# Choosing which partitions stay empty in a row gather with duplicates removed

## The chip, the cores and the metric

The kernel runs on one core of a Trainium2 chip. The metric is the device time of one execution in microseconds. The core has five compute or control engines, PE (TensorE), DVE (VectorE), ACT (ScalarE), POOL (GpSimd) and SP (SyncE), and 16 DMA engines that move data between HBM and the on-chip memory of 128 partitions.

## The reference

```python
def setup_inputs():
    batch, seq, dim = 32, 512, 1024
    return {
        "x": np.random.randn(batch, seq, dim).astype(np.float32),
        "indices": np.random.randint(0, seq, (batch, 128)).astype(np.int32),
    }

def reference(x, indices):
    result = np.zeros((batch, indices.shape[1], x.shape[2]), dtype=np.float32)
    for b in range(batch):
        result[b] = x[b, indices[b]]
    return result
```

For each of 32 batches, 128 rows of 1024 float32 (4 KB each) are copied from 512 rows, chosen by an index that may name a row more than once. The draw is fixed: batches have between 109 and 120 different rows among their 128, the last one (batch 31) 113.

## The kernel before, in words

The output is 32 blocks of 128 rows, one per batch, each written by a store of 512 KB that SP issues (`store`, L137 to L142; batches 12 to 19 are stored in pairs, 1 MB each). Input rows come by indirect DMAs that POOL issues (`gather`, L121, one per batch, 128 slots, one slot per partition).

Batches 0 to 4 (`HEAD`) are gathered directly, duplicates included, into `block` tiles and stored. Batch 0 takes its indices from `first`, a small transfer of one column; batches 1 to 4 take them from `idxT`, the transposed indices, which PE and DVE make out of `vals` by way of `vf` (L94 to L113).

Batches 5 to 31 are handled in nine groups of three. For these, each different row is fetched once. DVE and PE work out, in three steps per group (`step0`, `step1`, `step2`):

- `cnt`: how many earlier places in the batch name the same row. `lead` marks the places with none, that is the first mention of each row.
- `past` and `nth`: the running number of a leading place. It counts on through the batches, modulo 128, so that the run of numbers that a batch does not use moves on from batch to batch.
- `pack`: which partition (slot) takes which leading place. A slot p takes the place whose number equals `turn[p]`, a fixed permutation of 0 to 127 that is the same in all partitions and comes from the iotas of `rank` (L73 to L79, turned to float16 at L93).
- `at`: the row index that each slot fetches. A slot that no place claims gets 1024, beyond the limit of the gather's bounds check, and fetches nothing.
- `s`: a 0/1 matrix with which PE later spreads the fetched rows to all places that name them.

The gather for such a batch goes into one of eight ring tiles `u` (`RING`, L207 to L215; ACT clears them once at the start, since empty slots keep what is there). PE multiplies `s` with the tile in two halves of 512 columns, ACT copies each half from PSUM to the batch's block, and SP stores the block (`spread_rows`, L238 to L247). The gather eight batches later is then issued. Batch 5 also uses 256 rows that two plain loads (`early`) bring ahead; its gather fetches only rows from 256 on.

Each engine's instructions keep the order in which the code emits them: a helper (`InOrder`, L13 to L25) chains the operations of PE, DVE and ACT, which is why most rows of the profile carry L21 or L24. POOL and SP work through their DMA issues in order. Waits between engines are semaphores that the framework sets. The DMA engines serve the queues of stores (q1, issued by SP), gathers (q0, issued by POOL), the loads by ACT (q10) and two queues marked "instruction" (q8, q14).

Of the kernel before, what the change touches and what calls it, by code (L numbers as in the profile page):

```python
# [7 lines left out]
F16 = mybir.dt.float16  # L8
I32 = mybir.dt.int32
ALU = mybir.AluOpType  # L10
# [18 lines left out]
def kernel(ctx, tc, x, indices, out):  # L29
# [11 lines left out]

    nc = tc.nc
    B, S, D = x.shape
    N = indices.shape[1]
    HEAD, RING, GROUP, AHEAD, FAR = 5, 8, 3, 4, 1024
    HALF = HEAD
    PAIRED = range(12, 20)
    GROUPS = (B - HEAD) // GROUP  # L50
    assert 2 * N <= S <= FAR and (B - HEAD) % GROUP == 0
    const = ctx.enter_context(tc.tile_pool(name="const", bufs=1))
# [8 lines left out]
    pe, dve, act = InOrder(tc), InOrder(tc), InOrder(tc)  # L61
    mm, v = nc.tensor.matmul, nc.vector
# [7 lines left out]

    diff = const.tile([N, N], I32, name="diff")
    nc.gpsimd.iota(diff[:], pattern=[[1, N]], base=0, channel_multiplier=-1)
    rank = const.tile([N, 8, 16], I32, name="rank")  # L73
    for e in range(8):
        fold = 0
        for bit, col in enumerate((6, 5, 3)):
            fold ^= col * (e >> bit & 1)
        steps = [[(-16 if fold >> bit & 1 else 16) << bit, 2] for bit in (2, 1, 0)]
        nc.gpsimd.iota(rank[:, e], pattern=[[1, 2]] + steps, base=2 * e + 16 * fold, channel_multiplier=0)  # L79
    less = const.tile([N, 1], F32, name="less")  # L80
    zero = const.tile([N, 1], F32, name="zero")
    dve(v.memset, zero[:], 0.0)
# [6 lines left out]
    dve(v.tensor_copy, out=less[:], in_=diff[:, 0:1])  # L89
    every = const.tile([N, N], F16, name="every")  # L90
    dve(v.memset, every[:], 1.0)
    turn = const.tile([N, N], F16, name="turn")
    dve(v.tensor_copy, out=turn[:], in_=rank[:].rearrange("p e q -> p (e q)"))  # L93
    vf = const.tile([N, N], F16, name="vf")  # L94
    dve(v.memset, vf[:], 0.0)
    dve(v.tensor_copy, out=vf[:B],
        in_=vals[:].bitcast(I32).rearrange("p (n two) -> p n two", two=2)[:, :, 0])


    xf = x.flatten_outer_dims()  # L100
# [47 lines left out]
    def table(name, dtype):  # L148
        return const.tile([N, B], dtype, name=name)

    cnt, lead, slot = table("cnt", F32), table("lead", F16), table("slot", F16)
    nth, at = table("nth", I32), table("at", I32)
    past = const.tile([N, B + 1], F16, name="past")
    dve(v.memset, past[:, HEAD:HEAD + 1], 0.0)
    bcs, packs, spread = {}, {}, {}

    def of_group(g):
        return range(HEAD + g * GROUP, HEAD + (g + 1) * GROUP)

    def cols(t, g):  # L160
        return t[:, HEAD + g * GROUP:HEAD + (g + 1) * GROUP]

    def wide(t):
        return t.rearrange("p (g o) -> p g o", o=1).to_broadcast([N, GROUP, N])

    def step0(g):

        bcs[g] = bc = pbc.tile([N, 4, N], F32, name="bc")
        for k, b in enumerate(of_group(g)):
            pe(mm, bc[:, k], lhsT=ident[:, b:b + 1].to_broadcast([N, N]), rhs=vf[:], start=True, stop=True)  # L170
        for k, b in enumerate(of_group(g)):
            junk = junkp.tile([N, N], F16, name="junk")
            dve(v.scalar_tensor_tensor, out=junk[:], in0=bc[:, k], scalar=idxF[:, b:b + 1], in1=below[:],
                op0=ALU.is_equal, op1=ALU.mult, accum_out=cnt[:, b:b + 1])
        if HALF in of_group(g):
            c = slice(HALF, HALF + 1)
            dve(v.scalar_tensor_tensor, out=cnt[:, c], in0=idxF[:, c], scalar=2.0 * N, in1=cnt[:, c],
                op0=ALU.is_lt, op1=ALU.add)
        dve(v.tensor_scalar, out=cols(lead, g), in0=cols(cnt, g), scalar1=0.0, scalar2=None, op0=ALU.is_equal)
        for b in of_group(g):  # L180
            dve(v.tensor_tensor, out=past[:, b + 1:b + 2], in0=past[:, b:b + 1], in1=lead[:, b:b + 1], op=ALU.add)

    def step1(g):

        rk = psm.tile([N, GROUP], F32, name="rk")
        pe(mm, rk[:], lhsT=above[:], rhs=cols(lead, g), start=True, stop=False)
        pe(mm, rk[:], lhsT=every[:], rhs=cols(past, g), start=False, stop=True)
        dve(v.tensor_copy, out=cols(nth, g), in_=rk[:])
        dve(v.tensor_scalar, out=cols(nth, g), in0=cols(nth, g), scalar1=N - 1, scalar2=None, op0=ALU.bitwise_and)
        dve(v.scalar_tensor_tensor, out=cols(slot, g), in0=cols(cnt, g), scalar=256.0, in1=cols(nth, g),  # L190
            op0=ALU.mult, op1=ALU.add)
        packs[g] = pack = junkp.tile([N, GROUP, N], F16, name="pack")
        dve(v.tensor_tensor, out=pack[:], in0=turn[:].rearrange("p (o n) -> p o n", o=1).to_broadcast([N, GROUP, N]),
            in1=wide(cols(slot, g)), op=ALU.is_equal)

    def step2(g):

# [40 lines left out]
    def spread_rows(b):  # L238
# [8 lines left out]
        store(b)  # L247

    step0(0)
    step0(1)  # L250
    for g in range(AHEAD):
        step1(g)
        if 0 < g < AHEAD - 1:
            step0(g + 1)
        step2(g)
        for b in of_group(g):
            if b < HEAD + RING:
                fetch(b)
        if g == 0:
            half_spread()  # L260
        elif g < 3:
            half_rows(g - 1, False)
    for b in range(HEAD, B):
        spread_rows(b)
        fetch(b + RING)
        g, step = divmod(b - HEAD, GROUP)
        if g + AHEAD < GROUPS:
            (step0, step1, step2)[step](g + AHEAD)
# [30 lines left out]
```

## Time and profile before

| what | value |
|---|---|
| median of 9 runs | 88.55 us (87.98 to 89.06) |
| the profiled execution | 88.22 us |
| its span | 86.4 us |
| PE / DVE / ACT / POOL busy | 72% / 37% / 47% / 39% of the span |
| bytes moved by DMA | 32.91 MB, mean 381 GB/s |
| gathers of batches 5 to 31 | 27 issues, 11.7 us from issue to landing (median) |
| stores | 24 of 512 KB (9.2 us to landing), 4 of 1 MB (12.8 us) |

The span is the time from the first instruction to the end of the last one in the profiled execution; its own time also counts what lies around it. A busy share is an average over the whole span. The DMA row of the profile gives, for 40 equal slices, how much of the 16 DMA engines' time was taken, in tenths, and the GB/s row what they moved. The DMA queue rows give packets, megabytes and the time that the packets took as a share of 16 engines' span. In the tables by stretches, the columns are the stretch, its length, the busy time of PE, weight loads, DVE, ACT and POOL with the number of instructions, then PE's granted clock, the DMA share and GB/s. A timeline row has start, duration, engine, line, operation, what it writes and reads, and in brackets how long the engine had been idle before it and what ended that.

### The profile page before, as it was taken

The page shows a single profiled execution, that of the slowest core. Times are in us where ns is not written, and L with a number is a line of the kernel's source. Part 1 is how long each engine was busy: PE and PEld are TensorE (multiplying, and loading weights), DVE is VectorE, ACT ScalarE, POOL GpSimd, SP SyncE. Part 2 cuts the span into 40 slices and gives each one's busy share as a digit, 9 for nine tenths or more (in the row PEclk, how much of TensorE's full clock was granted, in tenths as well). Part 3 has the DMA queues.
Part 4 walks back from the last instruction along what each step waited for, and adds up shares of the span by engine and source line. Part 5 has one row for each costly group of instructions (what it writes and reads, how often), then busy time and mean ns, then how long its engine had stood idle before and what let it go on. Part 6 is the DMA issues. An engine that isn't in the chain of part 4 may idle for free.

```text
span 86.4 us, 829 instructions
## 1 busy us (share of the span) xinstructions
PE 61.9 (72%) x189; PEld 25.4 (29%) x189; DVE 31.6 (37%) x160; ACT 40.5 (47%) x63; POOL 33.5 (39%) x45
## 2 busy tenths in 40 slices
PE   0040169596799999999999999777798888785000
PEld 0030133151345444443444443222133333220000
DVE  3289895592565486473754850000000000000000
ACT  0999910000165665566566555555434454455000
POOL 7557587737144555554445555433200000000000
PEclk9999999999999999999999999999999999999955
DMA  0998999999999999999999999999999999999970
GB/s 1 256 408 271 328 334 336 415 421 419 415 415 421 421 419 419 415 421 417 419 417 410 415 423 421 421 419 413 417 423 421 413 419 419 421 419 421 417 324 9
DMA packets 9636, 32.91 MB, mean 381 GB/s; under 512 B 1584, under 2 KB 1616, under 8 KB 9632
## 3 DMA queue, kind: packets, MB, share of 16 engines
q1 hardware_dynamic: 4736, 16.81, 47.9%
q0 software_dynamic: 4608, 15.01, 44.6%
q10 hardware_dynamic: 288, 1.05, 3.4%
q8 instruction: 1, 0.02, 0.1%
q14 instruction: 3, 0.02, 0.1%
HBM read 17.86 MB, written 16.78 MB: 401 GB/s over the span
## 4 chain that ended last, share of the span: by engine, by line
PE 40%; DMA 23%; issue 13%; DVE 9%; POOL 5%; ACT 1%; POOLq 1%; SPq 0%; DVEq 0%
PE ps L24 38%; DMA u<-in_x_dram,at 19%; POOL u L122 5%; DMA vals<-in_indices_dram 3%; DVE junk L24 2%; DVE nth L24 1%; DVE pack L24 1%; DVE past L24 1%; PE pos L24 1%; PE bc L24 1%; DVE slot L24 1%; ACT block L246 1%; DVE s L24 1%; DVE same L24 1%; SPq L66 0%
## 5 line engine op out<-in xcount | busy, mean ns | idle before, releaser
L24 PE MATMUL ps<-u,s 128*128 128x512 f32 x108 | 51.9, 610 | 4.7 <-DMA u<-in_x_dram,at 4.6
L122 POOL DMA_INDIRECT u<-in_x_dram,at x27 | 26.9, 997 | 24.5 <-PE bc L24 6.1
L246 ACT COPY block<-ps 128x512 f32<-128x512 f32 x36 | 21.1, 585 | 18.4 <-PE ps L24 16.8
L24 PEld LDWEIGHTS ps<-u,s 128*128 128x128 f32 x108 | 18.3, 189 | 26.4 <-ACT block L246 14.7
L246 ACT COPY pair<-ps 128x512 f32<-128x512 f32 x16 | 9.4, 585 | 5.9 <-PE ps L24 4.2
L24 DVE SCALAR_TENSOR_TENSOR junk<-bc,idxF,below 128x128 f16<-128x128 f32 x27 | 8.0, 347 | 6.2 <-PE bc L24 6.2
L24 ACT COPY u<-zero 128x1024 f32<-128x1024 f32 x8 | 7.7, 1038 | 0.0
L24 PE MATMUL ps<-early,same 128*128 128x512 f32 x8 | 7.3, 1064 | 0.0
L236 ACT COPY block<-ps 128x512 f32<-128x512 f32 x2 | 1.2, 585 | 12.5 <-PE ps L24 12.5
L24 PE MATMUL pos<-near,pack 128*128 128x1 f16 x27 | 2.0, 167 | 5.5 <-DVE pack L24 3.3
L24 DVE TENSOR_TENSOR pack<-turn,slot 128x384 f16<-128x384 f16 x9 | 5.0, 558 | 0.3
L24 DVE TENSOR_TENSOR s<-bc,at 128x384 f32<-128x384 f32 x9 | 5.0, 558 | 0.3
L24 DVE TENSOR_TENSOR past<-past,lead 128x1 f16<-128x1 f16 x27 | 4.4, 164 | 0.9
L122 POOL DMA_INDIRECT block<-in_x_dram,idxT x4 | 3.8, 946 | 1.9 <-DVE past L24 1.0
L24 PEld LDWEIGHTS <-pack 128*128 128x128 f16 x27 | 1.7, 100 | 9.5 <-DVE pack L24 4.8
L24 PE MATMUL bc<-vf,ident 128*128 128x128 f16 x27 | 3.4, 256 | 1.3 <-issue 1.3
L24 PEld LDWEIGHTS <-ident 128*128 128x128 f16 x27 | 2.4, 111 | 4.2 <-issue 4.2
L21 PE MATMUL pos<-ident,vf 128*128 128x32 f16 x1 | 0.2, 207 | 4.2 <-DVE vf L24 4.2
L24 DVE TENSOR_SCALAR at<-pos 128x3 int32<-128x3 f32 x9 | 1.4, 160 | 4.2 <-PE pos L24 3.8
L24 PEld LDWEIGHTS ps<-early,same 128*128 128x128 f32 x8 | 2.4, 324 | 2.1 <-issue 2.1
L24 DVE CAST nth<-rk 128x3 int32<-128x3 f32 x9 | 1.4, 159 | 3.9 <-PE rk L24 3.2
L24 ACT ACT_TABLE_LOAD x1 | 1.3, 1283 | 2.2 <-DVE ident L24 2.2
(31 smaller groups left out, 18.0 us busy)
## 6 DMA issues: line engine op xcount, KB each, us to landing
out_dram<-block SPq DMA_DIRECT2D x24, 512.0 KB, 9.2
out_dram<-pair SPq DMA_DIRECT2D x4, 1024.0 KB, 12.8
early<-in_x_dram ACTq DMA_DIRECT2D x2, 512.0 KB, 3.8
u<-in_x_dram,at POOLq DMA_INDIRECT x27, 11.7
block<-in_x_dram,idxT POOLq DMA_INDIRECT x4
vals<-in_indices_dram SPq DMA_DIRECT2D x1, 32.0 KB
first<-in_indices_dram SPq DMA_DIRECT2D x1, 1.0 KB
block<-in_x_dram,first POOLq DMA_INDIRECT x1
```

The costliest lines, as they stand in the source:

```text
L21: self.last = do(*args, **kw)
L24: self.last = do(*args, **kw)
L122: nc.gpsimd.indirect_dma_start(out=dst, out_offset=None, in_=xf[:], in_offset=bass.IndirectOffsetOnAxis(ap=at, axis=0), element_offset=b * ...
L236: nc.scalar.copy(out=blocks[HALF][:, w], in_=ps[:])
L246: nc.scalar.copy(out=blocks[b][:, w], in_=ps[:])
```

## The change

Two things are done to the permutation, and a few small ones follow.

First, `turn` is made from another formula. The new `rank[:, 0]` gives partition p the number 64 * ((p >> 5) & 1) + 16 * (p & 3) + 8 * (p >> 6) + ((p >> 2) & 7): numbers that follow one another belong to different values of 8 * (p >> 6) + ((p >> 2) & 7). In the old one they belong to different values of p >> 3.

Second, the last batch has a permutation of its own, `rank[:, 1]`, and its counting restarts at 0 (`past` of batch 31 is cleared). Numbers 112 to 123 lie at partitions 36 to 47, numbers 124 to 127 at partitions 104 to 107. The batch uses numbers 0 to 112, so its 15 empty slots are partitions 37 to 47 and 104 to 107.

The eight iotas of 16 elements for `rank` become one of 128 and five of 36, 12, 56, 4 and 20. The conversion to `turn` is 256 wide instead of 128 and comes after `vf` instead of before it. A second column of `past` is cleared at the start, and two additions to `past` in the last group are left out. The last group's `pack` is made by two instructions, one for two batches and one for the last.

```diff
-    rank = const.tile([N, 8, 16], I32, name="rank")
-    for e in range(8):
-        fold = 0
-        for bit, col in enumerate((6, 5, 3)):
-            fold ^= col * (e >> bit & 1)
-        steps = [[(-16 if fold >> bit & 1 else 16) << bit, 2] for bit in (2, 1, 0)]
-        nc.gpsimd.iota(rank[:, e], pattern=[[1, 2]] + steps, base=2 * e + 16 * fold, channel_multiplier=0)
+    rank = const.tile([N, 2, N], I32, name="rank")
+    nc.gpsimd.iota(rank[:, 0], pattern=[[8, 2], [64, 2], [1, 8], [16, 4]], base=0, channel_multiplier=0)
+    for p0, p1, at0 in ((0, 36, 0), (36, 48, 112), (48, 104, 36), (104, 108, 124), (108, N, 92)):
+        nc.gpsimd.iota(rank[:, 1, p0:p1], pattern=[[1, p1 - p0]], base=at0, channel_multiplier=0)
...
-    turn = const.tile([N, N], F16, name="turn")
-    dve(v.tensor_copy, out=turn[:], in_=rank[:].rearrange("p e q -> p (e q)"))
     vf = const.tile([N, N], F16, name="vf")
...
+    turn = const.tile([N, 2, N], F16, name="turn")
+    dve(v.tensor_copy, out=turn[:], in_=rank[:])
...
-    dve(v.memset, past[:, HEAD:HEAD + 1], 0.0)
+    for b in (HEAD, B - 1):
+        dve(v.memset, past[:, b:b + 1], 0.0)
...
         for b in of_group(g):
-            dve(v.tensor_tensor, out=past[:, b + 1:b + 2], in0=past[:, b:b + 1], in1=lead[:, b:b + 1], op=ALU.add)
+            if b < B - 2:
+                dve(v.tensor_tensor, out=past[:, b + 1:b + 2], in0=past[:, b:b + 1], in1=lead[:, b:b + 1], op=ALU.add)
...
-        dve(v.tensor_tensor, out=pack[:], in0=turn[:].rearrange("p (o n) -> p o n", o=1).to_broadcast([N, GROUP, N]),
-            in1=wide(cols(slot, g)), op=ALU.is_equal)
+        like = GROUP - (g == GROUPS - 1)
+        dve(v.tensor_tensor, out=pack[:, :like], in0=turn[:, 0:1].to_broadcast([N, like, N]),
+            in1=wide(cols(slot, g))[:, :like], op=ALU.is_equal)
+        if like < GROUP:
+            dve(v.tensor_tensor, out=pack[:, like:], in0=turn[:, 1:2], in1=wide(cols(slot, g))[:, like:], op=ALU.is_equal)
```

## The prediction

> **What bounds the kernel now.** I read the slices and the DMA queues of the page first, then the busy time by stretches, then the stretches at the end, because a change of 15 transfer slots can only show where one DMA engine ends last.
>
> ```profile
> span 86.4 us, 829 instructions
> DMA  0998999999999999999999999999999999999970
> GB/s 1 256 408 271 328 334 336 415 421 419 415 415 421 421 419 419 415 421 417 419 417 410 415 423 421 421 419 413 417 423 421 413 419 419 421 419 421 417 324 9
> q1 hardware_dynamic: 4736, 16.81, 47.9%
> q0 software_dynamic: 4608, 15.01, 44.6%
> q8 instruction: 1, 0.02, 0.1%
> q14 instruction: 3, 0.02, 0.1%
> ```
>
> The DMA row is at 9 from the third slice to the last but one: the 16 engines together are the bound, and the 72% of PE is cover. q1 carries the stores, q0 the gathers. Two small queues carry instructions. The stretches say it in shares:
>
> ```profile
> 6.00:8.00 2.00, 0.33 (x2) 0.10 (x1) 1.79 (x13) 2.00 (x3) 1.53 (x2) 1.00 0.81 252
> 10.00:12.00 2.00, 0.48 (x3) 0.21 (x2) 1.90 (x8) 1.16 (x2) 1.12 (x2) 1.00 0.94 287
> 20.00:76.00 56.00, 50.38 (x151) 20.52 (x149) 18.48 (x86) 29.54 (x51) 20.51 (x21) 1.00 1.03 418
> ...
> 82.00:83.00 1.00, 0.00 (x0) 0.00 (x0) 0.00 (x0) 0.00 (x0) 0.00 (x0) 0.50 1.00 410
> 83.50:84.00 0.50, 0.00 (x0) 0.00 (x0) 0.00 (x0) 0.00 (x0) 0.00 (x0) 0.50 0.55 221
> 84.20:84.40 0.20, 0.00 (x0) 0.00 (x0) 0.00 (x0) 0.00 (x0) 0.00 (x0) 0.50 0.06 21
> 84.60:84.80 0.20, 0.00 (x0) 0.00 (x0) 0.00 (x0) 0.00 (x0) 0.00 (x0) 0.50 0.05 20
> 84.80:85.00 0.20, 0.00 (x0) 0.00 (x0) 0.00 (x0) 0.00 (x0) 0.00 (x0) 0.50 0.05 20
> ```
>
> The last two columns are DMA share and GB/s. From 20 to 76 us the share is 1.03 (records of one engine overlap a little), so no engine waits. At the end it falls to 0.05 to 0.06, which is 1/16: for most of a microsecond **one engine works alone**. The packet records behind these rows give the sixteen completion marks of the last store: fifteen between 83.30 and 84.31 us, the sixteenth at 85.19. The span ends 1.24 us after it.
>
> Why is one engine late? The DMA queues in 46 to 48 us, and in 38 to 40 us:
>
> ```profile
> q8 instruction: 1, 0.02, 2.9%
> q14 instruction: 1, 0.01, 1.0%
> ```
>
> 2.9% of 16 engines times 2 us is 0.93 us for one packet (16,384 bytes, 942 ns in the records); 1.0% is 0.32 us (8,192 bytes, 309 ns). Three of the latter lie in the span, at 14.2, 39.4 and 58.5 us. A 4 KB row costs 4096 bytes / (420 GB/s / 16) = 0.156 us, so the large fetch costs its engine six rows, a small one two. I followed each engine's packets by their end-to-start times (a packet starts 3 or 4 ns before the one ahead of it ends): the last engine's chain to the end begins where the 942 ns packet ends. A skipped slot shows there as a 4-byte packet of 9 ns instead of a 159 ns row.
>
> [...]of the final stretches that I could follow without a break, five match one engine (or a pair that it can't tell apart) exactly; dealing eight neighbouring partitions to each engine misses each by one to three. The 30 gather packets ahead of the 942 ns fetch fit engine 10 alone; those ahead of the fetch at 39.4 us fit engine 2 or 0. [...]
>
> **The change part by part.**
>
> *Ordinary batches.* Old and new `turn` both spread a run of up to 16 consecutive empty ranks over the engines. I counted, from the draw, the empty slots by engine: 432 in batches 5 to 31. The old table gives every engine 27. Before the last batch the new one gives 26 or 27. Nothing to gain here: 0.00 us; its cover is a ring of eight gathers, with the DMA share at 1.03.
>
> *The last batch.* It has 113 different rows of 128, so 15 empty slots. Old: one on each engine but 15. New: rank restarts at 0, ranks 113 to 127 lie at partitions 37 to 47 and 104 to 107, that is three on engine 1 and four each on 2, 3 and 10. Totals become 29 on engine 1, 30 on 2, 3 and 10, 27 on 15, 26 on the others. So engine 10 moves 30 - 27 = 3 rows less: 3 x 0.156 = **-0.47 us**. An engine with 26 moves one row more: +0.16. Is that the new end? The best of the rest ended at 84.31; plus 0.16 is 84.47, and engine 10 comes to 85.19 - 0.47 = 84.72. It stays last, so the whole 0.47 counts. The ceiling is 85.19 - 84.47 = 0.72.
>
> *The start.* The iotas of `rank` took 1.26 us for eight; now one of 128 elements (the `diff` iota let the next start after 0.20) and five at about 0.157: 0.99. POOL would be free at 2.03, not 2.30, but the first gather waits for the `first` transfer until 2.76: nothing. `turn` becomes 256 wide and moves behind `vf`, ahead of `idxT`:
>
> ```profile
> 2.33 0.23 DVE L24 CAST turn<-rank 128x128 f16<-128x128 int32 x1 [0.58 <-POOL rank L79]
> 3.94 0.21 DVE L24 CAST vf<-vals 32x128 f16<-32x128 int32 x1 [1.30 <-DMA vals<-in_indices_dram]
> 4.45 0.19 DVE L24 CAST idxT<-pos 128x32 int32<-128x32 f32 x1 [0.30 <-PE pos L21]
> 4.79 0.06 DVE L24 MEMSET past<- 128x1 f16 x1
> 4.91 0.95 POOL L122 DMA_INDIRECT block<-in_x_dram,idxT  x1 [1.03 <-DVE past L24]
> ```
>
> DVE idles 0.30 us ahead of `idxT`, waiting for PE. `below`, also 128 wide, let its successor start 0.14 after it, so 256 wide is about 0.28 of DVE; it begins between 4.08 and 4.15 and ends its claim at 4.36 to 4.43, just inside 4.45. Bounds: no delay, or 0.06 if only the record's end at 4.15 frees DVE and the full 0.36 counts. The second `past` memset costs 0.05 ahead of the first `junk`, so it delays `at`, the POOL gather queue behind it (first at 10.57) and the DMA engines. At 10 to 12 us these are at 0.94, not full, so a delay there can reach the end. Bounds 0.00 to 0.11; I take +0.03, as part of the engines still have work there.
>
> *The last group.* Its `pack` becomes two instructions (about +0.2 by the short DVE rows at 0.16 to 0.18), two `past` additions go (0.164 each). Its `at` is ready at 51.1 us and its gathers are issued from 55.0 on, when ring tiles and earlier gathers allow: nearly 4 us of cover, 0.00 us. Without it, at most 0.2.
>
> Sum: -0.47 + 0.03 = **-0.44 us**. The profiled execution, 88.22 us with a span of 86.4, would become 87.8; the median of the nine runs is 88.55, 0.33 above it, and would become **88.1**, 0.50% less. About 0.5%, or 0.44 us, is also what a measurement of this kernel can tell from no change.
>
> **The rivals.**
>
> *The late engine is not helped.* If the 16 KB fetch is on an engine outside the four, [...]that engine has 26 empties: +0.16 + 0.03, so 88.7. Against it: the fit to engine 10 and the nearly equal program length.
>
> *The start eats the gain.* If `turn` is dearer than its hole and delays all of the first gathers by 0.2 to 0.3, the result is 88.4. For it: the share of 0.81 at 6 to 8 us shows engines already starved by late gathers. Against it: the hole of 0.30.
>
> *Slower: gathers are dealt by eights.* If the software queue gives engine e the partitions 8e to 8e+7, the new `turn` gathers the empties of a batch on few engines, and totals run from 24 to 36. The last engine, if among the eight with 24, moves three rows more: 88.55 + 0.47 + 0.03 = 89.05. It decides from three rows on; with fewer it stays within 0.5%. [...]
>
> **How the numbers follow.** Relief of engine 10 has 0.66; its centre is on the bound of 0.5%, but a lag that is longer in other executions keeps the gain and a shorter start cost raises it, so 0.49 faster and 0.17 same; its own range is 87.8 to 88.4. Late engine not helped: 0.16 (0.14 same, 0.02 slower). Start eats: 0.10 (0.01 faster, 0.09 same). By eights: 0.08, slower. Sums: 0.50, 0.40, 0.10. The range reaches from the ceiling, 88.55 - 0.72 = 87.8, less 0.2 for the scatter of a median whose runs lie between 87.98 and 89.06, to 88.7 plus the same: 87.6 to 88.9.
>
> **What would show it.** Right: the last completion mark near 84.7, with the stretch at a share of 1/16 shortened from about 0.9 to about 0.25 us; `idxT` still at about 4.45 and the first gather of `u` within 0.1 of 10.57; the small queues still with one packet of 16 KB. Wrong: a lone engine as late as before, two or more engines beyond 84.5 with no large fetch, a steady share under 1.03, or gathers of batches 1 to 4 that begin 0.2 late.

## The result, and the profile after

The changed kernel takes 87.57 us (median of 10 runs, 87.18 to 87.95) beside 88.35 us for the kernel before (31 runs): ratio **0.992**, 95% interval 0.989 to 0.995, that is 0.7 us less (0.5 to 1.0). The forecast was 0.44 us less, 88.1 from 88.55. Ratios and intervals here leave out the executions that took over 1.5% longer than the fastest of the same kernel, so the tables also give the medians of all runs.

The forecast range, 87.6 to 88.9, was set from 88.55; the measured ratio puts 87.8 there, inside it (the median itself, 87.57, stands beside a kernel before at 88.35). Most of the reasoning behind the number did not hold, so that it came out is luck. The first sign is the profiled execution of the changed kernel, which took 88.28 us, no less than the 88.22 of before. Its page answers to the lines shown of before:

```profile
span 86.5 us, 827 instructions
DMA  0797899999999999999999999999999999999980
q8 instruction: 1, 0.02, 0.1%
q14 instruction: 3, 0.02, 0.1%
```

The same one large and three small instruction fetches, and a DMA row that is a little emptier at the start (7, 7 and 8 in the second, fourth and fifth slice, where it was 9, 8 and 9). Then the same stretches (columns as before: the last two are DMA share and GB/s):

```profile
6.00:8.00 2.00, 0.33 (x2) 0.10 (x1) 1.85 (x15) 2.00 (x3) 1.39 (x2) 1.00 0.81 236
20.00:76.00 56.00, 48.30 (x142) 19.94 (x143) 18.20 (x85) 28.13 (x48) 20.98 (x21) 1.00 1.03 418
...
84.20:84.40 0.20, 0.00 (x0) 0.00 (x0) 0.00 (x0) 0.00 (x0) 0.00 (x0) 1.00 0.55 225
84.80:85.00 0.20, 0.00 (x0) 0.00 (x0) 0.00 (x0) 0.00 (x0) 0.00 (x0) 0.50 0.05 20
```

The lone engine at the end (a share of 0.05) now lasts some 0.3 us instead of 0.9: the completion marks of the last store run from 83.93 to 84.80 us, and the sixteenth is at 85.11. So the end is more even, as forecast, though engine 10 is no longer the lone one: by its packets it ends at about 84.5. And the marks' mean is 84.38, against 83.95 before: this execution was already late when it got there. The timeline of its start shows why, and shows a row that the prediction had not asked about:

```profile
1.04 0.50 POOL L76 IOTA rank<- 128x128 int32 x1
1.10 0.48 DVE L24 TENSOR_SCALAR ident<-diff 128x32 f16<-128x32 int32 x1 [0.23 <-POOL diff L74]
1.61 0.38 ACTq L21 DMA_DIRECT2D early<-in_x_dram  x1
4.51 0.22 DVE L24 CAST vf<-vals 32x128 f16<-32x128 int32 x1 [2.46 <-DMA vals<-in_indices_dram]
5.03 0.19 DVE L24 CAST idxT<-pos 128x32 int32<-128x32 f32 x1
5.49 0.95 POOL L121 DMA_INDIRECT block<-in_x_dram,idxT  x1 [1.61 <-DVE past L24]
```

And the rows of the kernel before that answer to it and were not shown:

```profile
1.10 0.18 DVE L24 TENSOR_SCALAR ident<-diff 128x32 f16<-128x32 int32 x1 [0.23 <-POOL diff L72]
1.31 0.38 ACTq L21 DMA_DIRECT2D early<-in_x_dram  x1
```

`ident` takes 0.48 us instead of 0.18, since it runs beside the wide iota of 0.50 us; it ends at 1.58, just after the iota. ACT's `early` loads wait for `ident` (`mark`), so they are issued at 1.61 instead of 1.31. Two streams that meet there are the index block `vals` (32 rows of 1 KB, issued at 1.19) and these loads (4 KB rows). In this execution the block was used at 4.51 us, 0.6 later than in the profile of before: all its rows but one had landed by 2.6 us, and that one, which starts at 4.02 as a 4 KB row of the early loads ends, landed at 4.06. Below, a row like this is called caught. In another execution of the same kernel (the run that stands last below) it looks like this:

```profile
1.61 0.38 ACTq L21 DMA_DIRECT2D early<-in_x_dram  x1
2.97 0.21 DVE L24 CAST vf<-vals 32x128 f16<-32x128 int32 x1 [0.92 <-DMA vals<-in_indices_dram]
4.17 0.95 POOL L121 DMA_INDIRECT block<-in_x_dram,idxT  x1 [0.30 <-DVE past L24]
```

There `vf` starts at 2.97 instead of 3.94 and the gather of batch 1 at 4.17 instead of 4.91, when POOL is through with batch 0. That execution took 87.30 us. So there were two theories to tell apart. **L**: the gain is the relief of engine 10, as forecast. **S**: the gain is made at the start, by an iota that slows a DVE instruction that holds back a load.

### The profile page after: what moved, and what is told of

Read it like the earlier page. It is cut to its first block, busy times and chain, and to the rows that moved or that the text cites. A ratio compares the mean times of both kernels' runs of the same rounds, so it can differ in the third digit from the quotient of the medians.

```text
span 86.5 us, 827 instructions
## 1 busy us (share of the span) xinstructions
PE 61.2 (71%) x189; PEld 25.2 (29%) x189; DVE 31.6 (36%) x160; ACT 40.6 (47%) x63; POOL 33.4 (39%) x43
## 4 chain that ended last, share of the span: by engine, by line
DMA 41%; PE 17%; issue 16%; DVE 16%; POOL 3%; ACT 1%; SPq 0%; POOLq 0%; DVEq 0%
DMA u<-in_x_dram,at 37%; PE ps L24 15%; DVE junk L24 4%; DMA vals<-in_indices_dram 4%; POOL u L121 3%; DVE pack L24 3%; DVE past L24 2%; DVE s L24 2%; DVE nth L24 2%; DVE lead L24 1%; DVE slot L24 1%; ACT block L250 1%; PE pos L24 1%; DVE same L24 1%; SPq L68 0%
## 5 line engine op out<-in xcount | busy, mean ns | idle before, releaser
L24 PE MATMUL ps<-early,same 128*128 128x512 f32 x8 | 5.7, 854 | 0.0
L24 DVE TENSOR_TENSOR pack<-turn,slot 128x384 f16<-128x384 f16 (+2 forms) x10 | 5.1, 518 | 0.3
L24 PEld LDWEIGHTS ps<-early,same 128*128 128x128 f32 x8 | 1.9, 257 | 1.5 <-issue 1.5
```

Source lines behind the costliest of these rows:

```text
L24: self.last = do(*args, **kw)
```

## The experiments

**First four: move the empty slots of the last batch, leave the start as changed.** Each edit is to the second table of the changed kernel (the first shows both lines that go, the other two only what is new); the last run is the changed kernel itself.

```diff
# even: one empty slot on each engine but 0
-    for p0, p1, at0 in (...):
-        nc.gpsimd.iota(rank[:, 1, p0:p1], pattern=[[1, p1 - p0]], base=at0, channel_multiplier=0)
+    nc.gpsimd.iota(rank[:, 1], pattern=[[8, 2], [64, 2], [1, 8], [16, 4]], base=0, channel_multiplier=0)
# on engines 12 to 15 (in place of the same two lines)
+    nc.gpsimd.iota(rank[:, 1], pattern=[[1, N]], base=0, channel_multiplier=0)
# eight on engine 10
-    for p0, p1, at0 in ((0, 36, 0), (36, 48, 112), (48, 104, 36), (104, 108, 124), (108, N, 92)):
+    for p0, p1, at0 in ((0, 38, 0), (38, 45, 113), (45, 72, 38), (72, 76, 120), (76, 104, 65), (104, 108, 124), (108, N, 93)):
```

> The changed kernel with one thing undone: the last batch's 15 empty slots lie one on each DMA engine but engine 0 (the second table repeats the first). The new table of the ordinary batches, the wide conversion and its new place stay. Theory L (the gain is the relief of engine 10, which fetches 16 KB of instructions): no gain is left, ratio to the kernel before 1.000 within 0.003. Rival S (the gain comes from the start or from the new table of the ordinary batches): still about 0.992, as the changed kernel.

> The changed kernel, but the last batch's empty slots lie on engines 12 to 15 (3, 4, 4, 4), none on 1, 2, 3 and 10. Theory L: engine 10 moves one row more than before, +0.16 us, ratio about 1.002 and slower than the kernel with even slots. Rival C (bunching of empty slots helps wherever it is, for example by a shorter landing of the last gather): about 0.992, as the changed kernel.

> The changed kernel, but all eight slots of engine 10 are empty in the last batch, the other seven on engines 1 (2), 2 (4) and 3 (1). Theory L with a fixed order of the other engines: engine 10 ends 8 rows less 1, that is 1.09 us, earlier than with even slots and is no longer last; the end is that of the next engine, so a gain of at most about 0.7 us and ratio 0.990 to 0.992, at best 0.2 us better than the changed kernel. Rival (a straight dose): ratio 0.988.

> The changed kernel once more, on the same chip and with the same runs of before as the three others, for the comparison: 0.992, interval about 0.003 each way. Its trace tells how much of the late start of the profiled execution (index block there at 4.4 instead of 3.8 us) belongs to the change: theory J (scatter of the transfer) expects it near 3.8 us in at least some of the four traces, the rival (the wide iota delays it) at 4.4 in all four.

Measured against the kernel before:

| empty slots of the last batch | ratio | 95% interval | all runs: median us, its ratio to 88.43 |
|---|---|---|---|
| even | 0.9957 | 0.9931 to 0.9983 | 88.13, 0.997 (22 runs) |
| on 12 to 15 | 0.9915 | 0.9883 to 0.9946 | 87.65, 0.991 (8) |
| eight on 10 | 0.9905 | 0.9877 to 0.9934 | 87.99, 0.995 (22) |
| as changed, four on 10 | 0.9907 | 0.9870 to 0.9944 | 87.41, 0.988 (9) |

Theory L fails clearly on the second row: with no empty slot at all on engine 10 the kernel is as fast as with four, where L said slower than before. Eight are no better than four, so no dose of engine 10 is to be seen between none, four and eight. With even slots a gain of 0.4 us stays; L said none and S the whole gain, so this row fits neither. What all four share is the start. Their index blocks were in use at 3.17, 3.28, 4.33 and 3.23 us, so the 4.51 of the first profile was one of the two cases that occur, and the rival "4.4 in all four" fails too.

**Four more: both halves apart, on the kernel before.**

```diff
# last batch alone: a second table, made on POOL in the steady part; start and ordinary batches as before
+            for p0, p1, at0 in ((0, 36, 0), (36, 48, 112), (48, 104, 36), (104, 108, 124), (108, N, 92)):
+                with tc.issue_after(gathers[HEAD + RING].ins):
+                    nc.gpsimd.iota(rank2[:, 0, p0:p1], pattern=[[1, p1 - p0]], base=at0, channel_multiplier=0)
+            dve(v.tensor_copy, out=turn2[:], in_=rank2[:])
+            dve(v.memset, past[:, B - 1:B], 0.0)
... (declarations; and past as in the changed kernel)
+            dve(v.tensor_tensor, out=pack[:, like:], in0=turn2[:], in1=wide(cols(slot, g))[:, like:], op=ALU.is_equal)
# early loads later: wait for the fifth DVE operation instead of the second
-    mark = dve(v.tensor_scalar, out=ident[:], in0=diff[:, :B], scalar1=0, scalar2=None, op0=ALU.is_equal)
+    dve(v.tensor_scalar, out=ident[:], in0=diff[:, :B], scalar1=0, scalar2=None, op0=ALU.is_equal)
...
-    dve(v.tensor_copy, out=less[:], in_=diff[:, 0:1])
+    mark = dve(v.tensor_copy, out=less[:], in_=diff[:, 0:1])
# latest: mark is the copy to turn
```

> The kernel before with the last batch's own table alone (empty slots on engines 1, 2, 3 and 10 as in the changed kernel); the table is made late, in the steady part, so that the start, the narrow iotas and the ordinary batches are those of before. Theory L (the gain is the relief of engine 10): -0.47 us, ratio 0.995. Theory S (the gain is made at the start: the wide iota on POOL slows DVE's ident, the early loads are issued 0.3 us later, at 1.6 instead of 1.3, and the index block lands earlier): 1.000, as the start is that of before. Both together, each with half: 0.995 to 0.997.

> The kernel before with one edit: the early loads wait for the fifth DVE operation (the copy to less, done at about 1.6 us) instead of the second (ident, 1.28), so that they are issued about 0.3 us later, as in the changed kernel. Nothing of the dealing is changed. Theory S: the index block lands near 2.8 us in most executions, the gathers of batches 1 to 4 start up to 0.7 us earlier, ratio 0.994 to 0.996, like the kernel with even slots in the last batch. Theory L: 1.000.

> Both edits on the kernel before: the last batch's own table, made late, and the early loads 0.3 us later. If the gain of the changed kernel is the sum of these two, 0.991 to 0.993, as the changed kernel, with nothing left for the new table of the ordinary batches, the wide conversion or its place. If one of the two does all, as that one alone.

> A larger dose of the second edit: on the kernel before, the early loads wait for the copy to turn (done at about 2.56 us), so they are issued about 1.3 us later than before and mostly after the index block has landed. Theory S: the index block is at 2.8 us in every execution and the scatter of the times falls; the early loads themselves come 1.3 us later, which costs only if batch 5 is waiting for them. Ratio 0.992 to 0.996; 1.000 or more if the idle DMA time ahead of them, 1.0 us, is lost.

| edit on the kernel before | ratio | 95% interval | all runs: median us, its ratio to 88.34 |
|---|---|---|---|
| last batch alone | 0.9986 | 0.9953 to 1.0020 | 88.32, 1.000 (14 runs) |
| early loads 0.3 us later | 0.9878 | 0.9823 to 0.9933 | 87.80, 0.994 (6) |
| both | 0.9921 | 0.9894 to 0.9947 | 87.85, 0.994 (22) |
| early loads 1.3 us later | 1.0020 | 0.9998 to 1.0042 | 88.49, 1.002 (22) |

The dealing of the last batch, which was the whole forecast, is worth 0.1 us or nothing. One changed wait, in a kernel whose dealing is untouched, gives a gain (0.994 to 0.996 was expected of it). By the ratios it is the gain of the changed kernel; by the medians of all runs it is 0.5 us, where the changed kernel has 0.8 to 1.0 in its three measurements (0.991, 0.988, 0.989). Whether something else adds to it there, or rows are caught less often there, the runs do not show. The timelines of the second and the fourth show the mechanism and its other side:

```profile
1.64 0.38 ACTq L21 DMA_DIRECT2D early<-in_x_dram  x1
3.27 0.21 DVE L24 CAST vf<-vals 32x128 f16<-32x128 int32 x1 [0.64 <-DMA vals<-in_indices_dram]
4.25 0.95 POOL L122 DMA_INDIRECT block<-in_x_dram,idxT  x1 [0.37 <-DVE past L24]
```

```profile
2.60 0.38 ACTq L21 DMA_DIRECT2D early<-in_x_dram  x1
3.21 0.21 DVE L24 CAST vf<-vals 32x128 f16<-32x128 int32 x1 [0.58 <-DMA vals<-in_indices_dram]
4.19 0.95 POOL L122 DMA_INDIRECT block<-in_x_dram,idxT  x1 [0.31 <-DVE past L24]
```

In both the index block is in use by 3.3 us and the gathers of batch 1 start at 4.2. But with the loads at 2.60 the DMA engines have too little to do from 2 to 4 us. The stretches of the second kernel, then of the fourth:

```profile
2.00:4.00 2.00, 0.46 (x6) 0.46 (x7) 0.73 (x6) 1.45 (x2) 1.43 (x3) 1.00 0.69 238
6.00:8.00 2.00, 0.00 (x0) 0.00 (x0) 1.79 (x13) 2.00 (x3) 1.40 (x2) 1.00 0.91 299
```

```profile
2.00:4.00 2.00, 0.52 (x6) 0.52 (x7) 0.78 (x6) 0.51 (x1) 1.43 (x3) 1.00 0.29 56
6.00:8.00 2.00, 0.00 (x0) 0.00 (x0) 1.77 (x13) 2.00 (x3) 1.39 (x3) 1.00 1.02 401
```

The fourth loses (0.69 - 0.29) x 2 = 0.8 us of full DMA time before 4 us, and has 0.2 us more from 6 to 8 by the share, (401 - 299) x 2 / 420 = 0.5 us by the GB/s, at the 420 of the steady part. By 18 us 1258 of its 4 KB rows have landed, beside 1339 in the second kernel and 1286 in the kernel before. So the earlier block no longer pays: 0.3 us of delay for these loads was worth its price here, 1.3 us was not.

**The last four: undo only the slow `ident`, and take the cause away by other means.**

```diff
# narrow first: the changed kernel, its wide iota in four, the first two beside ident
-    nc.gpsimd.iota(rank[:, 0], pattern=[[8, 2], [64, 2], [1, 8], [16, 4]], base=0, channel_multiplier=0)
+    nc.gpsimd.iota(rank[:, 0, 0:16], pattern=[[1, 4], [16, 4]], base=0, channel_multiplier=0)
+    nc.gpsimd.iota(rank[:, 0, 16:32], pattern=[[1, 4], [16, 4]], base=4, channel_multiplier=0)
+    nc.gpsimd.iota(rank[:, 0, 32:64], pattern=[[1, 8], [16, 4]], base=64, channel_multiplier=0)
+    nc.gpsimd.iota(rank[:, 0, 64:128], pattern=[[64, 2], [1, 8], [16, 4]], base=8, channel_multiplier=0)
# index block on ACT's queue, ahead of the early loads (on the kernel before, and on the changed one)
-    nc.sync.dma_start(out=vals[:], in_=indices)
+    act(nc.scalar.dma_start, out=vals[:], in_=indices)
```

> The changed kernel with its first wide iota cut into four (16, 16, 32 and 64 elements), so that the DVE's ident runs beside narrow iotas again and the early loads are issued at 1.3 us as in the kernel before. The dealing of all batches, the last batch's own table and the wide conversion stay. Theory S (the gain comes from the later early loads): the index block lands at 3.4 us or later, ratio 0.997 to 1.000, like the kernel with the last batch's table alone. Theory L (dealing): still 0.992.

> The kernel before with one edit: the index block is loaded from ACT's queue ahead of the early loads, so that it is issued at about 0.75 us instead of 1.18; the early loads stay at 1.3. Theory S: the block is in before the first 4 KB rows start at 2.36, near 2.3 us; the gathers of batches 1 to 4 are then held by POOL alone (from 4.2), and no DMA time is given away for it: ratio 0.987 to 0.991. If the ordering of the early loads and not the index block mattered: 1.000.

> The changed kernel with the index block on ACT's queue ahead of the early loads; these stay delayed by the wide iota. Theory S: 0.987 to 0.991, no better than the kernel before with the same edit but for what the dealing is worth, at most 0.3 us (0.003), less 0.3 us of DMA time lost to the later early loads.

> The changed kernel once more, beside the three others for the comparison: 0.992, interval 0.003 each way; index block near 2.8 us, or near 4 us in the minority of executions in which one of its rows is caught behind the early loads.

| kernel | ratio | 95% interval | all runs: median us, its ratio to 88.66 |
|---|---|---|---|
| changed, narrow iotas first | 1.0007 | 0.9966 to 1.0047 | 88.53, 0.999 (14 runs) |
| before, index block on ACT's queue | 0.9928 | 0.9903 to 0.9953 | 87.86, 0.991 (22) |
| changed, index block on ACT's queue | 0.9858 | 0.9790 to 0.9926 | 87.41, 0.986 (6) |
| changed, again | 0.9927 | 0.9888 to 0.9967 | 87.67, 0.989 (12) |

The first row decides. That kernel keeps every slot of the changed one and differs from it in how one iota is cut, and the whole gain is gone. Its timeline has the old start again:

```profile
1.04 0.15 POOL L76 IOTA rank<- 128x16 int32 x1
1.10 0.18 DVE L24 TENSOR_SCALAR ident<-diff 128x32 f16<-128x32 int32 x1 [0.23 <-POOL diff L74]
1.31 0.38 ACTq L21 DMA_DIRECT2D early<-in_x_dram  x1
3.87 0.21 DVE L24 CAST vf<-vals 32x128 f16<-32x128 int32 x1 [2.05 <-DMA vals<-in_indices_dram]
```

And its stretch from 6 to 8 us, where gathers of batches 1 to 4 should keep the engines busy, beside that of the changed kernel in the last run:

```profile
6.00:8.00 2.00, 0.33 (x2) 0.10 (x1) 1.79 (x13) 2.00 (x3) 1.59 (x2) 1.00 0.84 236
```

```profile
6.00:8.00 2.00, 0.00 (x0) 0.00 (x0) 1.76 (x12) 2.00 (x3) 1.39 (x3) 1.00 0.97 356
```

By the share that is 0.13 x 2 = 0.26 us of full DMA time in this stretch alone, by the GB/s (356 - 236) x 2 / 420 = 0.57 us. Counting 4 KB rows that have landed by 18 us puts the whole start into one number. The three executions with the early loads at 1.3 us and the index block on SP's queue: 1286 (before), 1297 (last batch alone), 1265 (narrow iotas), mean 1283. Those with the loads at 1.6, the block on the same queue and no row caught: 1317 to 1375, mean 1341 of six. The difference of the means, 58 rows, is 58 x 0.156 / 16 = 0.57 us, the size of the gain. In the two executions where one row of the index block was caught behind the loads it is 1249, and the profiled times are 88.28 and 88.41 us: the gain is not had in every execution.

The index block on ACT's queue, in the kernel before:

```profile
0.74 0.40 ACTq L21 DMA_DIRECT2D vals<-in_indices_dram  x1
2.84 0.26 DVE L24 CAST vf<-vals 32x128 f16<-32x128 int32 x1 [0.21 <-DMA vals<-in_indices_dram]
4.28 0.95 POOL L122 DMA_INDIRECT block<-in_x_dram,idxT  x1 [0.30 <-DVE junk L24]
```

The block's last row lands at 2.27 us, and the gain is about the same without any help from a slow `ident` (0.9928; 0.987 to 0.991 was expected). The batch 1 gather still starts at 4.28, since POOL is busy with batch 0 until 3.97 and leaves 0.30 between gathers that follow at once, so landing before 2.8 us buys nothing more there. Together with the changed kernel's start and dealing it has the lowest ratio, 0.986 (87.41 us, interval 0.979 to 0.993); its 1416 rows by 18 us are the most. Its interval overlaps those of the other faster versions, so that it beats the changed kernel is not shown.

## Why the prediction was right in its number and wrong in its reason

**Engine 10 carries the large fetch, and the mapping of slots: right.** Following all 16 engines from 22.5 us to the end, the pattern of 4-byte packets leaves one engine (or a few that it can't tell apart) for each stream in the profile of before. Engine e is here the one whose packets fit the eight partitions p with 8 * (p >> 6) + ((p >> 2) & 7) = e. Six streams of that profile run for 100 to 237 gather packets with a single candidate at every step, and in each of them all packets, rows and empty slots, fall as the index draw puts them for one such e (in one of the six, for either of two); with eight neighbouring partitions to an engine the best fit of the six misses 7 to 24 packets. The 942 ns fetch is in engine 10's stream: the 129 gather packets ahead of it fit e = 10 alone. Engine 10 is the one that ends at 85.19. The fetches at 39.4 and 58.5 us are on engines 2 and 1.

**Three rows less move engine 10 by 0.47 us: right in kind.** Its end against the mean of the sixteen marks, in the executions that I could follow (with even slots, and with none on engine 10, the pattern leaves 9 or 10, and the stream with the large fetch is taken):

| empty slots on engine 10 | engine 10's end less the mean, us |
|---|---|
| none | 0.85 |
| one (before; even; index block on ACT's queue and early loads 1.3 us later on the kernel before) | 1.24, 1.41, 1.57, 0.91 |
| four (seven executions) | 0.14, 0.27, 0.70, 0.72, 0.77, 1.17, 1.41 |
| eight | 0.44 |

The means for one and four, 1.28 and 0.74, differ by 0.54, near the forecast of 0.47. But single executions scatter by more than that, and the one with none lies below the mean for one, so the size is not shown.

**"It stays last, so the whole 0.47 counts": this step failed.** I took the order of the other fifteen from one execution. Their ends move from execution to execution: in three of the seven with four slots another engine was last (4, 3 and 11), in the one with eight it was 4. In the kernel with the last batch alone, engine 3 had 400 rows left at 22.5 us where the mean was 390, and ended at 85.09, nearly as late as engine 10 before. The forecast's own sign of being wrong was there in the profile of the changed kernel, which came late from its start on: seven engines without the large fetch end beyond 84.5 us, and the gather of batch 1 begins 0.6 us later than before. The relief is thus there in the packets and worth 0.1 us (a gain of 0.4 to a loss of 0.2) in the time of the last-batch kernel, and nothing in the narrow-iota kernel (a gain of 0.3 to a loss of 0.4), both against a forecast of 0.44. Whether bunching the slots is worth something when the start is the faster one is open: even slots have 0.9957, four on engine 10 have 0.9907 to 0.9927, and slots on 12 to 15, which cannot relieve engine 10, 0.9915.

**"The start: +0.03": this step failed, in sign and in size.** The forecast left out a path: iota, `ident`, early loads, index block, gathers. Its two sums for POOL and DVE were near: the first gather waits for `first` until 2.77, the wide `turn` takes 0.27 and `idxT` starts 0.52 after `vf`, 0.51 before. What I left out is whom the wide iota hinders. I priced it by the `diff` iota at 0.20 and called the rest of POOL's time cover; it took 0.50, and `ident` beside it 0.48. In all seven profiled executions with the wide iota `ident` takes 0.48 us and ends 0.04 us after the iota; in all seven with iotas of about 0.16 in its place it takes 0.18. Why `ident` takes longer beside the wide iota is not shown. From there the chain is `ident`, `mark`, `early` loads, and these compete with `vals`. The prediction quoted the row in which `vf` waits 1.30 us for `vals`, and took the landing as given. It also read the DMA row as 9 from the third slice on; the fourth slice, 6.5 to 8.6 us, is at 8, and the last but one at 7.

**The rival "the start eats the gain"** had the place right (0.81 at 6 to 8 us shows engines starved by late gathers) and the sign wrong for most executions; in the two with a caught row the start did eat the gain. The last group's `pack` and `past` cost nothing that shows: the kernel with the last batch alone has both and is at 0.9986.

**The sum.** Forecast -0.47 and +0.03; measured about -0.1 for the dealing alone and about -0.7 for the start (1.0007 against 0.9927 at the same dealing; with both intervals, 0.2 to 1.2). A relief that did not reach the end and a gain that the forecast did not hold left a sum near it.

## What to carry to other kernels

When an edit touches the set-up, follow every instruction that runs beside it to what waits for it, loads on other queues too: here a slower DVE instruction of 0.3 us made the kernel faster, since it kept large rows out of the way of a small transfer on which all gathers but the first hang (`vals` in use at 2.97 instead of 3.94 us). Issuing the small transfer first, on a queue that was free, gave about the same gain and does not hang on the slow instruction. And an engine that is late in one execution is a reason to look at several before its lag is counted as time: what comes next can be as late in another, as here in four of the eight executions with four or eight empty slots on engine 10.

## What the runs showed of the hardware that I had not expected

- The 1 KB rows of `vals` took longer where 4 KB rows met them on the DMA engines: the 32 rows took 169, 179 and 108 ns each in the mean in the three executions with the early loads at 1.3 us, single ones up to 1132 while half of them took under 56, and 47 to 68 in the mean where the early loads came 0.3 us later. In two executions of eight with the later loads a single row landed 1.4 to 1.5 us after the rest.
- An iota of 128 elements over four levels of pattern took 0.50 us, one over a single level 0.22 to 0.28 (`diff`, and the plain second table); 16 elements took 0.15 to 0.17.
- The engines with instruction fetches lost more than the packets' time: beyond its rows and the 0.94 us packet, engine 10's stream has 0.5 to 0.6 us more than most others, engines 1 and 2 about 0.3 us beyond their 0.31. In the profile of before, engines 10 and 15 both moved 391 rows after 22.5 us and ended at 85.19 and 83.65; of these 1.54 us the packet is 0.94.
